# The first modulation on VectorE and rows of TensorE, and a first product that begins with half its channels

## The chip, the cores and the metric

The kernel runs on one core of a Trainium2 chip. The metric is device time in microseconds (us). Three timed runs of the kernel before gave 3132.72, 3133.52 and 3138.29; their median is 3133.52 us. One more execution was profiled, and all rows below are of that one. Engines are named as in the profile: PE is TensorE (PEld its weight loads), DVE is VectorE, ACT is ScalarE, POOL is GpSimd, SP is SyncE, which issues the loads. A line number such as L418 is that of the kernel before.

## The reference

Two transformer blocks run over 512 tokens of 1024 channels. Only the first steps of the first block matter here:

```
mod = silu(c) @ w_ada + b_ada            # w_ada: 1024 x 6144
sh1, sc1, g1, sh2, sc2, g2 = split(mod, 6)
h = layer_norm(x) * (1 + sc1) + sh1
z, xbc, dt, ... = split(h @ w_in, ...)   # the mixer's first product
```

All of it is float32. `sh1` and `sc1` are the first 2048 of the 6144 columns of `mod`: a vector of 1024 numbers times a matrix of 1024 x 2048, 8 MB of weights. After it come the mixer (a state-space scan and a short convolution), an expert layer, and the second block.

## The kernel before

**Layout.** `hT` holds the modulated activations with channels on partitions: eight chunks k of 128 channels by 512 tokens. For exactness each float32 operand of a big product is split into a high part `hi` and a rest `lo`, and a product is three matmuls (L220 to L222: hi by hi, lo by hi, hi by lo). `split` (L191, L192) makes them: ACT casts, and DVE (or another engine, `eng`) subtracts. `W.get` loads a weight block in two halves of 512 KB into `raw` (3 buffers) and splits each; a half holds four of the eight chunks. `lin_a(w, m, act)` adds up the eight chunks of 128 output channels: 24 matmuls of 128 x 512.

**The first stage** (L385 to L509) is a scope in which the order on DVE, ACT, POOL and PE is the order in which the program writes the operations; SP's loads and all that comes after the scope are placed by a planner. The stage takes statistics of the four token tiles of x, normalises each and turns it with PE transposes into `xnT` (`turn_x`), computes `sh1` and `sc1`, modulates (`modulate`: `hfull` on DVE or POOL, `hhi` on ACT, then `hlo` on DVE) and computes the first product, two times `lin_a` with the same weights (`first`, L495).

**The modulation's matrix** is worked off in four units of 512 columns, class `Ada`, in the order 0, 2, 1, 3. Units 0 and 2 give shift and scale of chunks 0 to 3, units 1 and 3 those of chunks 4 to 7. A unit loads its 1024 x 512 weights as four tiles of 512 KB (`w_ada`, 8 buffers); a tile has two of the eight chunks of rows. `part(n)` takes a tile: of the eight chunks, three are scaled by ACT and summed by POOL (`suma`), four are summed by DVE (`sumb`, L416 and L418), and one (the seventh) goes to PE straight. PE adds over the partitions with small matmuls that have 128 weights by 128 columns as the loaded operand and one column moving (`columns`, L425; four, which show as eight instructions, per tile or sum). `total` does so for the two sums, and `end` adds the three contributions on DVE (L436) and the bias (L438).

The units are interleaved: `total` and `end` of a unit stand behind `part(0)` and `part(1)` of the next (L478 to L489). Chunks 0 to 3 are modulated in the turn in which unit 1 is the new one (`j == 1`), after unit 2's `end`. Chunks 4 to 7 follow the last `end`, and then PE has the whole first product. Its weights' rest `lo` is subtracted on POOL (`eng=G`, L491).

Later, units of the remaining modulation are done beside the mixer; of these, some end in a row product (L320: one weight column, 512 columns moving).

Of the kernel before, what the change touches and what calls it, by code (L numbers as in the profile page):

```python
# [10 lines left out]
F32 = mybir.dt.float32  # L11
# [3 lines left out]
AF = mybir.ActivationFunctionType  # L15
OP = mybir.AluOpType
# [8 lines left out]
KT = 8  # L25
# [113 lines left out]
def body(tc, ins, out, stop=None, dump=None):  # L139
# [10 lines left out]
    def dma(dst, src):  # L150
        return nc.sync.dma_start(dst, src)

    with top:
# [4 lines left out]
        def psum(tag="mm", bufs=4, shape=(128, 512)):  # L158
            return pp.tile(list(shape), F32, tag=tag, bufs=bufs, name=tag)
# [34 lines left out]
        class W:  # L194
            def __init__(self, st, raw=3, hl=4, own=True, **kw):
                self.p = pool(st, "wts", **kw)
                self.rp = self.p if own is True else own.rp
                self.raw, self.hl = raw, hl

            def half(self, src, eng=V):  # L200

                r = self.rp.tile([128, 1024], F32, tag="raw", bufs=self.raw, name="raw")
                dma(r, src)
                hi = self.p.tile([128, 1024], F32R, tag="hi", bufs=self.hl, name="hi")
                lo = self.p.tile([128, 1024], F32R, tag="lo", bufs=self.hl, name="lo")
                split(r, hi, lo, eng)
                return hi, lo

            def get(self, src, n=KT, eng=V):

                out = [], []
                c = 2048 // n
                for a in range(2):
                    for t, o in zip(self.half(src[:, a * 1024:(a + 1) * 1024], eng), out):
                        for k in range(n // 2):
                            o.append(t[:, k * c:(k + 1) * c])
                return out

        def mm3(ps, lh, ll, rh, rl, start, stop):
# [4 lines left out]
        def lin_a(w, m, act, nk=KT, ps=None, k0=0, stop=True):  # L224

            ps = psum() if ps is None else ps
            for k in range(k0, nk):
                s = slice(m * 128, (m + 1) * 128)
                mm3(ps, w[0][k][:, s], w[1][k][:, s], act[0][k], act[1][k], k == 0,
                    stop and k == nk - 1)  # L230
            return ps
# [153 lines left out]
        with ExitStack() as st:  # L385
            p = pool(st, "p0", side="right")
            E = mybir.EngineType
            st.enter_context(tc.manual_schedule(engines={E.DVE, E.Activation, E.Pool, E.PE}))
            x0 = []
            for i in range(NT):  # L390
                t = p.tile([128, D], F32, name=f"x{i}")
                dma(t, ins["x"][i * 128:(i + 1) * 128, :])
                x0.append(t)

            class Ada:


                def __init__(self, j):
                    self.j, self.raw, self.n = j, [], 0
                    for n in range(4):  # L400
                        self.raw.append(p.tile([128, 2, 512], F32, name="w_ada", bufs=8))
                        dma(self.raw[n], ins["w_ada"][j, n // 2][:, n % 2 * 2:n % 2 * 2 + 2, :])
                    self.sums = [p.tile([128, 512], F32, name="sum" + n, bufs=2) for n in "ab"]

                def part(self, n):
                    (a, b), r = self.sums, self.raw[n]
                    for k in range(2):
                        c, x = cs1[:, n * 2 + k:n * 2 + k + 1], r[:, k, :]
                        if n * 2 + k == 6:
                            self.columns(x, c)  # L410
                        elif k == 0 and n < 3:
                            S.activation(x if n else a, x, AF.Copy, scale=c)
                            if n:
                                G.tensor_add(a, a, x)
                        elif n == 0:
                            V.tensor_scalar(b, x, c, None, op0=OP.mult)  # L416
                        else:
                            V.scalar_tensor_tensor(b, x, c, b, op0=OP.mult, op1=OP.add)  # L418

                def columns(self, x, c):  # L420

                    if not self.n:
                        self.ps = psum("sm", 2)
                    for a in range(4):
                        PE.matmul(self.ps[:, self.n * 4 + a:self.n * 4 + a + 1],  # L425
                                  x[:, a * 128:(a + 1) * 128], c, start=True, stop=True)
                    self.n += 1

                def total(self):
                    for t in self.sums:  # L430
                        self.columns(t, ones[:, 0:1])

                def end(self):
                    j = self.j
                    dst = (sc1 if j > 1 else sh1)[:, j % 2 * 4:j % 2 * 4 + 4]
                    V.tensor_reduce(dst, self.ps[:, :self.n * 4].rearrange("p (n a) -> p a n", a=4),  # L436
                                    AX.X, OP.add)
                    V.scalar_tensor_tensor(dst, dst, float(j > 1), bcol1[:, j * 4:(j + 1) * 4],  # L438
                                           op0=OP.add, op1=OP.add)

            mvs = p.tile([128, NT, 2], F32, name="mvs")
            for i in range(NT):
                st_ = p.tile([128, 2, 6], F32, name="bn0", bufs=2)
                for a in range(2):
                    V.bn_stats(st_[:, a, :], x0[i][:, a * 512:(a + 1) * 512])
                V.bn_aggr(mvs[:, i, :], st_)
            rs = rsqrt(p, mvs[:, :, 1], NT, 1.0, LN_EPS)
            xnT = p.tile([128, KT, T], F32, name="xnT")

            def turn_x(i):  # L450
                xn = p.tile([128, D], F32, name="xn0", bufs=2)
                V.tensor_scalar(xn, x0[i], mvs[:, i, 0:1], rs[:, i:i + 1],
                                op0=OP.subtract, op1=OP.mult)
                for kh in range(2):
                    ps = psum("tr", 2)
                    for k in range(4):
                        PE.transpose(ps[:, k * 128:(k + 1) * 128],
                                     xn[:, (kh * 4 + k) * 128:(kh * 4 + k + 1) * 128], ident)
                    S.copy(xnT[:, kh * 4:kh * 4 + 4, i * 128:(i + 1) * 128],
                           ps.rearrange("p (k t) -> p k t", k=4))  # L460

            def modulate(k):
                f = p.tile([128, T], F32, name="hfull", bufs=3)
                a, b = sc1[:, k:k + 1], sh1[:, k:k + 1]
                (G if k % 2 else V).tensor_scalar(f, xnT[:, k, :], a, b, op0=OP.mult, op1=OP.add)
                S.activation(hhi[k], xnT[:, k, :], AF.Identity, scale=a, bias=b)
                return f

            def modulated(ks):
                fs = [modulate(k) for k in ks]  # L470
                for k, f in zip(ks, fs):
                    V.tensor_sub(hlo[k], f, hhi[k].bitcast(F32))

            u = Ada(0)
            for n in range(4):
                u.part(n)
                turn_x(n)
            for j in (2, 1, 3):  # L478
                last, u = u, Ada(j)
                u.part(0)  # L480
                last.total()
                u.part(1)
                last.end()
                u.part(2)
                if j == 1:
                    modulated((0, 1))
                u.part(3)
                if j == 1:
                    modulated((2, 3))  # L489
            u.total()  # L490
            first_w = w.get(ins["w_in"][0], eng=G)  # L491
            u.end()
            modulated((4, 5))
            modulated((6, 7))
            first = [lin_a(first_w, a, hT) for a in range(2)]  # L495

            cw = sc_p.tile([128, 32, 5], F32, name="cw")
            dma(cw, ins["conv_w"])
            nrm = sc_p.tile([128, 16], F32, name="nrm")
            dma(nrm, ins["ssd_norm"])  # L500
            hd = sc_p.tile([128, 2, 32], F32, name="hd")
            load_row(hd[:, 0, :], ins["ssd_dt_bias"])
            load_row(hd[:, 1, :], ins["ssd_A_log"])
            wdt = p.tile([128, KT, 32], F32, name="wdt")
            dma(wdt, ins["w_dt"])
            V.tensor_scalar_mul(cw, cw, 0.5)
            wdh = sc_p.tile([128, KT, 32], F32R, name="wdh")
            wdl = sc_p.tile([128, KT, 32], F32R, name="wdl")
            split(wdt, wdh, wdl)  # L509
# [674 lines left out]
        with ExitStack() as st:  # L1184
# [38 lines left out]
            def rows(e):  # L1223
                return G.value_load(cnt[0:1, e:e + 1], min_val=0, max_val=T)
# [747 lines left out]
```

## Time and profile before

| | us |
|---|---|
| median of three timed runs | 3133.52 |
| the profiled execution | 3115.28 |
| its span, first to last instruction | 3113.3 |
| busy in the span: PE | 2872.3 |
| DVE | 2119.6 |
| ACT | 1501.2 |
| POOL | 856.5 |

The busy times are shares of the whole span and say little about a stage. The stage of the change takes the first 62 us; a table of stretches and the timeline of each engine show what it waits for. In a timeline a row gives start, duration, engine, line, operation, output and inputs, and in brackets how long the engine had been idle and what ended that. Rows of the same kind in a run are merged (x8), and durations of neighbours on an engine overlap a little.

### The profile page before, as it was taken

What the parts mean: (1) busy time and instruction counts of PE and PEld (TensorE: products, weight loads), DVE (VectorE), ACT (ScalarE), POOL (GpSimd) and SP (SyncE); (2) the same over time, 40 slices, a digit from 0 to 9 for tenths busy, and PEclk for the clock granted to TensorE, in tenths of its full rate; (3) what the DMA queues carried; (4) which work ended last, traced back from release to release, by engine and by line L of the source; (5) the groups of instructions that cost most, each with busy time, mean ns of one, the idle gap of its engine ahead of it and who ended that gap; (6) DMA issues with size and microseconds to landing.
All of it is one profiled execution on the core that took longest, in us unless ns stands there. A gap on an engine that the chain in (4) does not pass through costs nothing. (4 is left out here: it accounts for less than half of the span.)

```text
span 3113.3 us, 42594 instructions
## 1 busy us (share of the span) xinstructions
PE 2872.3 (92%) x14412; PEld 2356.3 (76%) x14412; DVE 2119.6 (68%) x3694; ACT 1501.2 (48%) x2524; POOL 856.5 (28%) x792
## 2 busy tenths in 40 slices
PE   6999999999878999889999399998999999899998
PEld 5888887887767777777777377687888877688886
DVE  7887887455587988786767668665555664774445
ACT  4443342455327877686666344644333425652222
POOL 3212212478352323232222402423100231310002
PEclk8999999999989999999999699999999998999999
DMA  6212414576448999998989323313333374232221
GB/s 240 81 69 97 161 67 155 200 241 227 146 150 290 323 320 327 315 334 274 308 282 292 105 92 113 105 65 138 135 122 109 103 257 147 84 129 94 89 88 68
DMA packets 143492, 540.45 MB, mean 174 GB/s; under 512 B 24320, under 2 KB 37632, under 8 KB 118528
## 3 DMA queue, kind: packets, MB, share of 16 engines
q1 hardware_dynamic: 106832, 422.21, 38.2%
q0 software_dynamic: 36272, 113.48, 13.0%
q8 instruction: 193, 3.16, 0.4%
q14 instruction: 195, 1.60, 0.2%
HBM read 509.43 MB, written 36.35 MB: 175 GB/s over the span
## 5 line engine op out<-in xcount | busy, mean ns | idle before, releaser
L192 DVE TENSOR_TENSOR lo<-raw,hi 128x1024 fp32r<-128x1024 f32 x679 | 841.7, 1266 | 337.0 <-ACT hi L191 329.8
L191 ACT CAST hi<-raw 128x1024 fp32r<-128x1024 f32 x697 | 715.9, 1053 | 576.4 <-PE mm L222 228.0
L221 PE MATMUL mm<-hlo,hi 128*128 128x512 f32 (+1 forms) x1400 | 517.3, 370 | 7.4 <-DVE hlo L962 7.4
L220 PE MATMUL mm<-hhi,hi 128*128 128x512 f32 (+1 forms) x1400 | 521.9, 373 | 1.7 <-ACT hhi L961 1.4
L222 PE MATMUL mm<-hhi,lo 128*128 128x512 f32 (+1 forms) x1400 | 517.0, 369 | 4.9 <-DVE lo L192 4.9
L220 PEld LDWEIGHTS mm<-hhi,hi 128*128 128x128 f32 x1400 | 269.4, 192 | 51.3 <-issue 5.2
L221 PEld LDWEIGHTS mm<-hlo,hi 128*128 128x128 f32 x1400 | 269.3, 192 | 50.8 <-DVE hlo L962 7.6
L222 PEld LDWEIGHTS mm<-hhi,lo 128*128 128x128 f32 x1400 | 269.0, 192 | 49.5 <-DVE lo L192 6.7
L220 PE MATMUL mm<-hi,xh 128*128 128x512 f32 x584 | 235.9, 404 | 16.2 <-ACTq L1415 8.2
L222 PE MATMUL mm<-hi,xl 128*128 128x512 f32 x584 | 231.9, 397 | 1.2 <-DVE xl L1265 1.2
L221 PE MATMUL mm<-lo,xh 128*128 128x512 f32 x584 | 229.9, 394 | 0.0
L355 POOL TENSOR_TENSOR ada_acc<-ada_acc,ada_w 128x512 f32<-128x512 f32 x112 | 168.4, 1504 | 212.0 <-ACT ada_acc L353 171.1
L220 PE MATMUL mm<-hi,fh 128*128 128x512 f32 x512 | 200.6, 392 | 5.6 <-ACT fh L191 3.4
L221 PE MATMUL mm<-lo,fh 128*128 128x512 f32 x512 | 200.4, 391 | 2.6 <-DVE lo L192 2.6
L222 PE MATMUL mm<-hi,fl 128*128 128x512 f32 x512 | 200.4, 391 | 0.0
L1220 POOL DMA_INDIRECT Rd<-ey,tt x73 | 121.7, 1667 | 242.8 <-ACT ey L1302 72.6
L1215 POOL DMA_INDIRECT x<-h2d,tt x69 | 92.2, 1337 | 333.9 <-PE mm L221 132.7
L220 PE MATMUL mm<-hi,hhi 128*128 128x256 f32 (+1 forms) x512 | 161.5, 315 | 7.3 <-ACT k L1864 7.3
L1809 DVE TENSOR_TENSOR res<-mm,gr 128x512 f32<-128x512 f32 x64 | 44.2, 691 | 180.5 <-PE mm L222 180.5
L222 PE MATMUL mm<-hi,hlo 128*128 128x256 f32 (+1 forms) x512 | 162.4, 317 | 0.0
L221 PE MATMUL mm<-lo,hhi 128*128 128x256 f32 (+1 forms) x512 | 160.6, 314 | 0.0
L220 PE MATMUL mm<-hi,ah 128*128 128x512 f32 x338 | 142.1, 420 | 6.8 <-ACT ah L1289 4.3
(815 smaller groups left out, 5860.1 us busy)
## 6 DMA issues: line engine op xcount, KB each, us to landing
raw<-in_w_gu SPq DMA_DIRECT2D x128, 1024.0 KB, 7.6
raw<-in_w_dn SPq DMA_DIRECT2D x64, 1024.0 KB, 7.5
raw<-in_mlp_w SPq DMA_DIRECT2D x128, 512.0 KB, 3.5
raw<-in_w_in SPq DMA_DIRECT2D x88, 512.0 KB, 3.6
ada_w<-in_ada_w POOLq DMA_DIRECT2D x64, 512.0 KB, 4.7
ada_w<-in_w_ada POOLq DMA_DIRECT2D x64, 256.0 KB, 3.3
ada_w<-in_ada_w POOLq DMA_DIRECT2D x64, 256.0 KB, 4.5
raw<-in_b_w_in SPq DMA_DIRECT2D x24, 512.0 KB, 4.8
```

Of the source, the lines that this page charges most:

```text
L191: S.copy(hi, raw)
L192: eng.tensor_sub(lo, raw, hi.bitcast(F32))
L220: PE.matmul(ps, lh, rh, start=start, stop=False)
L221: PE.matmul(ps, lh, rl, start=False, stop=False)
L222: PE.matmul(ps, ll, rh, start=False, stop=stop)
L355: G.tensor_add(acc, acc, x)
L1215: G.indirect_dma_start(out=buf[0:n, :], out_offset=None, in_=h2d, in_offset=index(b, e, n), bounds_check=T - 1, oob_is_err=False)
L1220: G.indirect_dma_start(out=Rd, out_offset=index(b, e, n), in_=y[0:n, :], in_offset=None, compute_op=OP.add)
L1809: V.tensor_mul(t[:, c], ps[n], g[:, c])
```

## The change

A unit no longer uses ACT and POOL. DVE sums the first five chunks into one tile (`asum`). PE takes the sum and the other three chunks with row products: one column of weights, 512 columns moving, four products into one PSUM row. `end` copies that row to SBUF with ACT, turns it into four columns with four PE matmuls of one partition, and adds the bias on DVE. `w_ada` has 10 buffers.

The order is changed too. Each unit's `end` stands right behind its last part. The halves of the first weights are loaded after the first two units' tiles and ahead of those of units 1 and 3, and are split with DVE in place of POOL, one half between the modulations of chunks 0, 1 and 2, 3, the other behind unit 1's parts. The first product is done in two pieces: chunks 0 to 3 (12 matmuls for each of the two outputs) around unit 3's first parts, chunks 4 to 7 at the end. `W.half` is divided into `load` and `halves`, with no other effect.

```diff
+                    self.sum = p.tile([128, 512], F32, name="asum", bufs=2)
+
+                def row(self, c, x, stop=False):
+                    start = self.ps is None
+                    if start:
+                        self.ps = psum("sm", 2)
+                    PE.matmul(self.ps[0:1, :], c, x, start=start, stop=stop)
 
                 def part(self, n):
...
+                    for k in range(n * 2, n * 2 + 2):
+                        c, x = cs1[:, k:k + 1], self.raw[n][:, k % 2, :]
+                        if k == 0:
+                            V.tensor_scalar(self.sum, x, c, None, op0=OP.mult)
+                        elif k < 5:
+                            V.scalar_tensor_tensor(self.sum, x, c, self.sum, op0=OP.mult, op1=OP.add)
                         else:
...
+                            if k == 6:
+                                self.row(ones[:, 0:1], self.sum)
+                            self.row(c, x, stop=k == 7)
+
+                def end(self):
+
+                    j = self.j
+                    r = p.tile([1, 512], F32, name="arow", bufs=2)
+                    S.copy(r, self.ps[0:1, :])
+                    q = psum("tr", 2)
                     for a in range(4):
...
+                        PE.matmul(q[:, a:a + 1], r[0:1, a * 128:(a + 1) * 128], ones[0:1, 0:1],
+                                  start=True, stop=True)
                     dst = (sc1 if j > 1 else sh1)[:, j % 2 * 4:j % 2 * 4 + 4]
...
+                    V.scalar_tensor_tensor(dst, q[:, :4], float(j > 1), bcol1[:, j * 4:(j + 1) * 4],
                                            op0=OP.add, op1=OP.add)
...
-            u = Ada(0)
+            u0, u2 = Ada(0), Ada(2)
             for n in range(4):
-                u.part(n)
+                u0.part(n)
                 turn_x(n)
-            for j in (2, 1, 3):
-                last, u = u, Ada(j)
-                u.part(0)
-                last.total()
-                u.part(1)
-                last.end()
-                u.part(2)
-                if j == 1:
-                    modulated((0, 1))
-                u.part(3)
-                if j == 1:
-                    modulated((2, 3))
-            u.total()
-            first_w = w.get(ins["w_in"][0], eng=G)
-            u.end()
+            u0.end()
+            raw = [w.load(ins["w_in"][0][:, a * 1024:(a + 1) * 1024]) for a in range(2)]
+            u1, u3 = Ada(1), Ada(3)
+            for n in range(4):
+                u2.part(n)
+            u2.end()
+            first_w = [], []
+            modulated((0, 1))
+            w.rows(first_w, w.halves(raw[0]), KT)
+            modulated((2, 3))
+            for n in range(4):
+                u1.part(n)
+            w.rows(first_w, w.halves(raw[1]), KT)
+            u1.end()
+            first = [lin_a(first_w, 0, hT, nk=4, stop=False)]
+            for n in range(4):
+                u3.part(n)
+                if n == 1:
+                    first.append(lin_a(first_w, 1, hT, nk=4, stop=False))
+            u3.end()
             modulated((4, 5))
             modulated((6, 7))
-            first = [lin_a(first_w, a, hT) for a in range(2)]
+            first = [lin_a(first_w, a, hT, ps=first[a], k0=4) for a in range(2)]
```

## Rows read from the trace of the kernel before

**Rows 1.** The page: busy time of the engines, and the span in 40 slices (busy tenths of PE).

```profile
PE 2872.3 (92%) x14412; PEld 2356.3 (76%) x14412; DVE 2119.6 (68%) x3694; ACT 1501.2 (48%) x2524; POOL 856.5 (28%) x792
...
PE   6999999999878999889999399998999999899998
```

**Rows 2.** The table of stretches: from and to, length, busy time (and instructions) of PE, PEld, DVE, ACT and POOL, granted clock, busy share of the DMA engines, GB/s.

```profile
26.00:48.50 22.50, 14.10 (x64) 13.84 (x65) 19.91 (x20) 8.35 (x12) 16.00 (x10) 0.51 0.72 245
48.50:54.00 5.50, 5.50 (x14) 4.34 (x15) 4.79 (x11) 4.41 (x8) 4.16 (x5) 0.50 0.03 7
54.00:62.30 8.30, 8.30 (x38) 6.68 (x37) 5.63 (x9) 2.77 (x3) 0.67 (x2) 1.00 0.62 198
62.30:840.00 777.70, 766.31 (x3918) 635.52 (x3917) 549.56 (x947) 321.37 (x521) 290.01 (x304) 0.99 0.43 147
```

**Rows 3.** The list of waits, of 14 to 54 us and, last, of PE from 55 to 840 us: who waited for whom, us in total, times, the longest.

```profile
PE sm L425 <- DVE sumb L418: 6.1, 2, 5.6
...
DVE sc L436 <- PE sm L425: 2.0, 1, 2.0
...
DVE sh L436 <- PE sm L425: 1.1, 1, 1.1
...
PE sm L320 <- DVE ada_acc L290: 4.2, 2, 2.3
```

**Rows 4.** The timeline of DVE in the first stage, with one row of ACT ahead.

```profile
12.18 0.72 ACT L412 ACTIVATE suma<-w_ada,cs 128x512 f32<-128x512 f32 x1 [8.35 <-DMA w_ada<-in_w_ada]
...
15.00 0.48 DVE L416 TENSOR_SCALAR sumb<-w_ada,cs 128x512 f32<-128x512 f32 x1
15.39 0.81 DVE L452 TENSOR_SCALAR xn<-x,mvs,rs_y 128x1024 f32<-128x1024 f32 x1
...
31.82 0.16 DVE L438 SCALAR_TENSOR_TENSOR sc<-sc,bcol 128x4 f32<-128x4 f32 x1
...
33.21 1.51 DVE L472 TENSOR_TENSOR hlo<-hfull,hhi 128x512 fp32r<-128x512 f32 x2
...
39.73 2.57 DVE L416 TENSOR_SCALAR sumb<-w_ada,cs 128x512 f32<-128x512 f32 x1
42.34 2.71 DVE L418 SCALAR_TENSOR_TENSOR sumb<-w_ada,cs,sumb 128x512 f32<-128x512 f32 x1
...
45.16 0.16 DVE L438 SCALAR_TENSOR_TENSOR sh<-sh,bcol 128x4 f32<-128x4 f32 x1
45.24 1.53 DVE L418 SCALAR_TENSOR_TENSOR sumb<-w_ada,cs,sumb 128x512 f32<-128x512 f32 x2
...
48.94 0.16 DVE L438 SCALAR_TENSOR_TENSOR sc<-sc,bcol 128x4 f32<-128x4 f32 x1
...
49.98 1.47 DVE L472 TENSOR_TENSOR hlo<-hfull,hhi 128x512 fp32r<-128x512 f32 x2 [0.30 <-ACT hhi L466]
...
52.01 1.51 DVE L472 TENSOR_TENSOR hlo<-hfull,hhi 128x512 fp32r<-128x512 f32 x2
```

**Rows 5.** The timeline of POOL.

```profile
39.39 5.11 POOL L192 TENSOR_TENSOR lo<-raw,hi 128x1024 fp32r<-128x1024 f32 x2
...
52.33 1.84 POOL L278 DMA_DIRECT2D ada_w<-in_w_ada  x3
```

**Rows 6.** The timeline of PE and of its weight loads.

```profile
18.04 1.57 PEld L457 LDWEIGHTS tr<-cst,xn 128*128 128x128 f32 x8 [0.22 <-ACT xnT L459]
...
21.86 0.94 PEld L457 LDWEIGHTS tr<-cst,xn 128*128 128x128 f32 x8
...
22.88 0.95 PE L425 MATMUL sm<-cst,suma 128*128 128x1 f32 x8
...
24.58 1.03 PE L425 MATMUL sm<-cs,w_ada 128*128 128x1 f32 x8
...
28.01 1.86 PE L425 MATMUL sm<-cst,suma 128*128 128x1 f32 x8 [2.40 <-POOL suma L414]
...
48.56 0.77 PE L220 MATMUL mm<-hhi,hi 128*128 128x512 f32 x1
...
55.50 0.40 PE L220 MATMUL sm<-hhi,wdh 128*32 128x512 f32 x1
...
62.10 0.39 PE L222 MATMUL mm<-hhi,lo 128*128 128x512 f32 x1
```

**Rows 7.** The row product of the later modulation, L320: the line's instructions (duration in ns, least, median and largest) and two of them in the timeline.

```profile
L320 PE MATMUL sm<-ada_acc,cst x32: 589/591/617, 293.5 to 2589.4; 128*1 128x512 f32 x32
...
293.46 1.02 PE L320 MATMUL sm<-ada_acc,cst 128*1 128x512 f32 x2
```

**Rows 8.** Groups by line in the first 60 us: busy time, mean ns of one, idle time before them.

```profile
L459 ACT COPY xnT<-tr 128x512 f32<-128x512 f32 x8 | 4.5, 586 | 5.3 <-PE tr L457 5.2
...
L192 DVE TENSOR_TENSOR lo<-raw,hi 128x1024 fp32r<-128x1024 f32 x2 | 2.5, 1226 | 0.2 <-ACT hi L191 0.2
...
L414 POOL TENSOR_TENSOR suma<-suma,w_ada 128x512 f32<-128x512 f32 x8 | 11.3, 1420 | 22.0 <-ACT w_ada L412 21.3 <-POOL suma L414 0.5
```

**Rows 9.** The table of stretches again, 2 us each, columns as in rows 2.

```profile
10.00:12.00 2.00, 0.00 (x0) 0.00 (x0) 1.97 (x5) 0.00 (x0) 0.00 (x0) 1.00 1.02 410
...
26.00:28.00 2.00, 0.00 (x0) 0.00 (x0) 1.97 (x2) 1.49 (x3) 1.92 (x3) 0.66 1.01 383
...
32.00:34.00 2.00, 2.00 (x11) 2.00 (x11) 1.90 (x3) 1.92 (x3) 1.49 (x1) 0.50 0.96 309
```

More of the change, by code (lines that the diff above doesn't have):

```diff
@@ L198, in __init__, with load, half, halves @@
                 self.raw, self.hl = raw, hl
-            def half(self, src, eng=V):
+            def load(self, src):
                 r = self.rp.tile([128, 1024], F32, tag="raw", bufs=self.raw, name="raw")
                 dma(r, src)
+                return r
+            def half(self, src, eng=V):
+                return self.halves(self.load(src), eng)
+            def halves(self, r, eng=V):
                 hi = self.p.tile([128, 1024], F32R, tag="hi", bufs=self.hl, name="hi")
@@ L207, in half, with rows @@
                 return hi, lo
+            def rows(self, out, ts, n):
+                c = 2048 // n
+                for t, o in zip(ts, out):
+                    for k in range(n // 2):
+                        o.append(t[:, k * c:(k + 1) * c])
             def get(self, src, n=KT, eng=V):
                 out = [], []
-                c = 2048 // n
                 for a in range(2):
-                    for t, o in zip(self.half(src[:, a * 1024:(a + 1) * 1024], eng), out):
-                        for k in range(n // 2):
-                            o.append(t[:, k * c:(k + 1) * c])
+                    self.rows(out, self.half(src[:, a * 1024:(a + 1) * 1024], eng), n)
                 return out
@@ L398, in __init__ @@
                 def __init__(self, j):
-                    self.j, self.raw, self.n = j, [], 0
+                    self.j, self.raw, self.ps = j, [], None
                     for n in range(4):
-                        self.raw.append(p.tile([128, 2, 512], F32, name="w_ada", bufs=8))
+                        self.raw.append(p.tile([128, 2, 512], F32, name="w_ada", bufs=10))
                         dma(self.raw[n], ins["w_ada"][j, n // 2][:, n % 2 * 2:n % 2 * 2 + 2, :])
-                    self.sums = [p.tile([128, 512], F32, name="sum" + n, bufs=2) for n in "ab"]
@@ L405, in part @@
-                def part(self, n):
[L406 to L416, printed above, removed]
-                        else:
-                            V.scalar_tensor_tensor(b, x, c, b, op0=OP.mult, op1=OP.add)
@@ L420, in columns @@
[L420 to L431, printed above, removed]
+                    self.sum = p.tile([128, 512], F32, name="asum", bufs=2)
@@ L433, in end @@
                 def end(self):
                     j = self.j
+                    r = p.tile([1, 512], F32, name="arow", bufs=2)
+                    S.copy(r, self.ps[0:1, :])
+                    q = psum("tr", 2)
+                    for a in range(4):
+                        PE.matmul(q[:, a:a + 1], r[0:1, a * 128:(a + 1) * 128], ones[0:1, 0:1],
+                                  start=True, stop=True)
                     dst = (sc1 if j > 1 else sh1)[:, j % 2 * 4:j % 2 * 4 + 4]
-                    V.tensor_reduce(dst, self.ps[:, :self.n * 4].rearrange("p (n a) -> p a n", a=4),
-                                    AX.X, OP.add)
@@ L438, in end @@
-                    V.scalar_tensor_tensor(dst, dst, float(j > 1), bcol1[:, j * 4:(j + 1) * 4],
+                    V.scalar_tensor_tensor(dst, q[:, :4], float(j > 1), bcol1[:, j * 4:(j + 1) * 4],
                                            op0=OP.add, op1=OP.add)
```

## The prediction

> **What bounds the kernel now.** I read the page first: PE is busy 92% of the span, and its slices are at 8 or 9 from the second on, but for two [rows 1]. A table by stretch then shows that this begins at 48.5 us: from 62.3 to 840 us PE works 766.3 of 777.7 us [rows 2]. So a microsecond by which the mixer's first product comes later should come out as a microsecond of the span, and all that counts is when PE gets through that product. Only the first 62 us are touched by the change. There PE is not the limit: from 26 to 48.5 us it works 14.1 of 22.5 us, at a granted clock of 0.51, while DVE works 19.9 and POOL 16.0 [rows 2].
>
> In the list of waits the reader should see that each unit's end hands over twice: PE waits for the sums (6.1 us, two waits), and DVE waits for PE (`sc` 2.0 us, `sh` 1.1) [rows 3]. DVE's waits are short, because it has operations of the next unit between a unit's sum and its end. The DVE timeline shows what DVE pays instead: a scale that takes 0.48 us at 15.0 takes 2.57 at 39.73, and a fused multiply-add that takes 0.74 at 45.24 (two in 1.53) takes 2.71 at 42.34 [rows 4], just beside the two splits on POOL, 39.39 to 44.50 [rows 5]. The last modulation column is written at 49.1 us [rows 4]. PE starts the first product at 48.56 [rows 6], 0.42 us a matmul at half clock until 54 (13 and a column matmul in 5.5 us), then 0.22 (38 in 8.3) [rows 2], and issues its 48th at 62.10; one matmul of the dt product (55.50) stands among them [rows 6]. The product is through at 62.3, or 62.1 without that one. I use 0.23 below, for the gaps between outputs.
>
> **The change, part by part.** The span is 3113.3 and the profiled execution 3115.3 us, 2.0 more; the sum is made against 3115.3. I lay out the new order on each engine, since DVE, ACT, POOL and PE take their instructions there as written.
>
> *Prices.* A unit's sum on DVE is one scale and four dependent multiply-adds: 0.52 + 4 x 0.78 = 3.64 us (durations of 0.48 and 0.74 plus 0.04 between dependent ones, [rows 4]), without POOL beside it. A row product (one column of weights, 512 fp32 columns moving) exists at L320: each product is two instructions of 0.59, which overlap (two in 1.02, so 0.43 apart): 0.86 us a product at full clock [rows 7]. At half clock the trace has none; the mixer's matmuls go from 0.22 to 0.42 [rows 2], about double, so 1.72. The four little matmuls that turn the row into columns are eight instructions, as those of L425: 0.95 us at full, 1.86 at half clock [rows 6]. The copy of the row from PSUM: 0.59, as L459 [rows 8]. The tail of a unit, from its sum to its written column, is then 3 rows + copy + columns + addition (0.16) + some 0.5 for five hand-overs: 2.6 + 0.6 + 0.95 + 0.16 + 0.5 = 4.8 us at full clock, 8.3 at half, 7.3 with the rows at half and the columns at full.
>
> *What it adds: a wait on DVE at each unit's end.* The addition in `end()` now stands on DVE in front of the next unit's sum, and it waits for rows, copy and columns. Everything of DVE queues behind it, and PE and ACT wait for DVE.
> - Unit 0: DVE starts at 15.0 as before; its sum is there at 15.0 + 3.64 + two normalisations of 0.73 = 20.1, the other two are done at 21.6. PE still has a row, 8 transposes, three rows and 8 transposes: 4 x 0.86 + 2 x 0.95 = 5.3 from 20.5, so 25.8; the last copy of transposes, the row's copy and the columns make it 28.3. DVE stands idle for 6.6 us.
> - Unit 2: sum at 28.3 + 3.6 = 32.0. PE has only one row to do from 28.1 and then nothing for 3 us; I let the clock fall there (below): tail 7.3, column at 39.3. Before: 31.98 [rows 4].
> - Chunks 0 to 3 and the first split: 2.7 us for two chunks as from 31.98 to 34.72 [rows 4], 1.2 for the split, 2.0 for the next two: 5.9, so 45.1. Unit 1: sum at 48.7, tail 7.3 (the second split, 1.2, lies under it): 56.0. Before: 45.3.
> - PE then does 24 matmuls of the first product, 24 x 0.23 = 5.5, and unit 3's four rows, 3.4, before the copy, columns and addition (2.0): last column at 66.7. DVE's sum of unit 3 (56.0 to 59.7) is hidden under the 24 matmuls.
> - The rest: before, hlo of chunks 4 and 5 was done 2.4 us after the last column, that of 6 and 7 4.4 us after it (49.1 to 51.45 and 53.52 [rows 4]); then 3 matmuls of chunk 7 and the 12 of the second output: 4.4 + 15 x 0.23 = 7.9. The product is through at 66.7 + 7.9 = 74.6.
>
> *What it removes.* ACT's scalings of 0.72 [rows 4], POOL's 8 additions of 1.42 [rows 8] and its two splits, 5.1 together [rows 5], all with the slowing of DVE, and 96 column instructions of PE. These savings are in the times above already, since I took DVE's undisturbed durations; DVE takes over the two splits at 1.23 each [rows 8].
>
> *Loads.* The bytes are the same. Tiles of 512 KB come at 410 GB/s, 1.27 us each (the DMA engines are full, 1.02, from 10 to 12 us), and at worst at 309 GB/s, 1.7 us (32 to 34) [rows 9]. The first tile is taken at 12.18 [rows 4], so 16 tiles and the two halves of `w_in` have landed by 12.2 + 17 x 1.27 = 33.8, at worst 41. The halves now stand in SP's queue ahead of units 1 and 3 and land by some 24 us. With 10 buffers the eleventh tile waits for unit 0's first (16.4), the last two for unit 2's first two (30.5). DVE wants unit 1 at 45 and unit 3 at 56: hidden, with over 4 us to spare; if that cover went, each late tile would cost 1.3 to 1.7. The small loads behind them in SP's queue come at about the times of before.
>
> *The clock.* It is 1.00 early on, 0.66 in 26 to 28 and 0.50 in 32 to 34 [rows 9]; it fell with the column matmuls over at 25.6 and PE idle till 28.0 [rows 6], stayed at half under more column matmuls, and was full again from 54, after some 5 us of mixer matmuls [rows 2]. The new order leaves PE idle from 29 to 32 and from 40 to 48.7, so I put the rows of units 2 and 1 at half clock and what follows at full. If it never fell, units 2 and 1 would have tails of 4.8 and the product would be through at 69; if it stayed low to the end of unit 3's rows, some 7 us more than mine.
> The Trainium skill (TensorE: Matmul & The Clock Gate, HAM oscillation) says that idle gaps between bursts of matmuls let the clock fall back to half, which speaks against this order; rows 9 agree, and by it the sum is mine, 74.6. The same page (Part 4: PE-mode transpose) says that transposes do not count as busy for the clock; here eight transpose loads took 1.57 us at 18.04 and 0.94 at 21.86 with little but transposes between [rows 6], so the measurement decides and unit 0's rows are at full clock; by the rule unit 0 would end 3.4 later.
>
> *Sum.* 74.6 - 62.1 = +12.5 us: 3115.3 + 12.5 = 3127.8, +0.40%. The three timed runs have a median of 3133.5, 18.2 above the profiled one; with the same shift that gives 3146.0. The two bounds: clock never low, 69 - 62 = +7; clock low throughout, about +20. On its way to the end the shift could shrink: PE has 11.4 us of idle between 62.3 and 840 [rows 2], the longest for `ada_acc` (4.2, two waits [rows 3]), whose loads start after this stage, at 52.33 [rows 5], and shift with it. I take all of it, with 4 as what could be swallowed.
>
> **Rivals.**
> - *Overlap (faster).* If DVE were not held at the ends (units' ends taken behind the next sums, as before), the four sums, the normalisations, the 5.9 us of chunks 0 to 3 with a split, and the other split make 15.0 + 14.6 + 2.9 + 5.9 + 1.2 = 39.6, a last tail of 4.8 gives 44.4, and the product is through at 52.3: -9.8 us, 3123.7 on the timed scale. For it: DVE's slowed operations go. Against: the order is written, and DVE's trace of before follows it exactly, even into waits [rows 3, 4]. It decides by the time for which DVE is held beyond that: under 9.8 us in all the change is faster, over that slower; I count 22.
> - *Holes refilled or clock kept (same).* The planner may put matmuls of the second weight block on chunks 0 to 3 (24 x 0.23 = 5.5 us) into PE's holes; with the clock kept up as well the rest is +7 - 5.5 = +1.5, 3135. For it: one dt matmul was pulled ahead at 55.50 [rows 6]. Against: PE's 5.6 us hole of before [rows 3] was not filled.
> - *Clock low throughout:* over +20, 3154 and more.
>
> **Chances.** Forecast (+6.3 to +20) 0.67, low clock beyond it 0.10, same 0.16, faster 0.07. A difference of 0.2%, 6.3 us, is about what can be told from none: slower 0.77, same 0.16, faster 0.07. The range, +0.5 to +20 us, is 3134 to 3154: it leaves out about a tenth on either side, the overlap below and the low clock above. The forecast alone has 3140 to 3154.
>
> **What would show it.** DVE idle of about 6 us before the addition of unit 0's `end()` and as much at units 2 and 1; the modulation's columns written at about 28, 39, 56 and 67 us; a granted clock of 0.5 in part of 29 to 55; PE's first product starting near 56, seven microseconds later than before, and through near 75. It is wrong if the DVE queue takes the next unit's sum before the addition, if a row product takes far from 0.86 or 1.72 us, or if the mixer starts late and the span doesn't follow.

## The result, and the profile after

The changed kernel takes 3150.53 us (median of 6 runs, 3145.28 to 3158.72), the kernel before 3130.09 beside it (6 runs, 3121.01 to 3138.29): a ratio of 1.0063, 95% interval 1.0044 to 1.0082. It is slower, as forecast, and 3150.5 lies inside the range; the forecast of 3146.0 was 4.5 us low. The profiled execution took 3147.95 us (span 3145.9).

The page of the changed kernel answers to [rows 1]: PE's share of the span is 92% again, so the page alone doesn't show where the time is.

```profile
PE 2881.3 (92%) x14380; PEld 2345.1 (75%) x14380; DVE 2117.5 (67%) x3696; ACT 1497.4 (48%) x2516; POOL 837.5 (27%) x782
```

The table of stretches does; first the three of [rows 2], then shorter ones (from and to, length, busy time and instructions of PE, PEld, DVE, ACT and POOL, granted clock, DMA share, GB/s).

```profile
26.00:48.50 22.50, 9.96 (x33) 3.13 (x31) 11.54 (x18) 8.59 (x13) 2.22 (x2) 0.70 0.52 177
48.50:54.00 5.50, 4.51 (x6) 0.60 (x6) 4.56 (x7) 0.41 (x1) 0.00 (x0) 0.50 0.43 107
54.00:62.30 8.30, 7.58 (x34) 5.47 (x34) 3.57 (x6) 0.86 (x2) 0.00 (x0) 0.92 0.35 125
...
28.00:30.00 2.00, 1.87 (x10) 0.92 (x10) 1.01 (x3) 0.00 (x0) 0.00 (x0) 1.00 0.91 363
30.00:32.00 2.00, 0.00 (x0) 0.00 (x0) 1.89 (x4) 0.00 (x0) 0.00 (x0) 0.87 0.33 102
32.00:38.00 6.00, 5.28 (x6) 0.59 (x6) 0.66 (x1) 0.00 (x0) 0.00 (x0) 0.50 0.80 234
...
42.00:54.00 12.00, 4.51 (x6) 0.60 (x6) 10.67 (x15) 4.91 (x7) 0.97 (x1) 0.50 0.32 94
...
56.00:62.00 6.00, 6.00 (x29) 4.88 (x29) 3.57 (x6) 0.00 (x0) 0.00 (x0) 1.00 0.16 65
```

From 26 to 48.5 us DVE was busy for 19.9 us before and for 11.5 after, POOL for 16.0 and for 2.2, PE for 14.1 and for 10.0: all three do less, and the stage is longer. From 32 to 38 us six instructions of PE at a clock of 0.50 are all that the core computes, but for the end of DVE's sum. The timeline of DVE says why (the bracket is its idle time before the instruction and what ended it):

```profile
28.96 0.16 DVE L443 SCALAR_TENSOR_TENSOR sh<-tr,bcol 128x4 f32<-128x4 f32 x1 [7.33 <-PE tr L440]
29.04 0.48 DVE L425 TENSOR_SCALAR asum<-w_ada,cs 128x512 f32<-128x512 f32 x1
29.55 3.11 DVE L427 SCALAR_TENSOR_TENSOR asum<-w_ada,cs,asum 128x512 f32<-128x512 f32 x4
39.74 0.16 DVE L443 SCALAR_TENSOR_TENSOR sc<-tr,bcol 128x4 f32<-128x4 f32 x1 [7.08 <-PE tr L440]
40.02 0.55 DVE L470 TENSOR_SCALAR hfull<-xnT,sc,sh 128x512 f32<-128x512 f32 x1
...
46.33 3.11 DVE L427 SCALAR_TENSOR_TENSOR asum<-w_ada,cs,asum 128x512 f32<-128x512 f32 x4
...
56.58 0.16 DVE L443 SCALAR_TENSOR_TENSOR sh<-tr,bcol 128x4 f32<-128x4 f32 x1 [3.45 <-PE tr L440]
56.66 0.48 DVE L425 TENSOR_SCALAR asum<-w_ada,cs 128x512 f32<-128x512 f32 x1
...
67.88 0.16 DVE L443 SCALAR_TENSOR_TENSOR sc<-tr,bcol 128x4 f32<-128x4 f32 x1 [3.55 <-PE tr L440]
```

L443 is the addition in `end()`. DVE stands idle in front of it at every unit. What follows at once had been queued behind it: L425, the next unit's first operation, at units 0 and 1, and the modulation of chunks 0 to 3 (L470) at unit 2. The list of waits of 14 to 80 us adds the four up, to 21.4 us, where [rows 3] has 3.1:

```profile
DVE sh L443 <- PE tr L440: 10.8, 2, 7.3
DVE sc L443 <- PE tr L440: 10.6, 2, 7.1
```

And PE's timeline is the other side of each wait:

```profile
32.72 1.86 PE L418 MATMUL sm<-asum,cst 128*1 128x512 f32 x2 [2.85 <-DVE asum L427]
34.38 3.62 PE L418 MATMUL sm<-w_ada,cs 128*1 128x512 f32 x4
38.66 1.05 PE L440 MATMUL tr<-cst,arow 1*128 1x1 f32 x8 [0.66 <-ACT arow L437]
...
49.49 1.87 PE L418 MATMUL sm<-asum,cst 128*1 128x512 f32 x2 [8.84 <-DVE asum L427]
...
56.47 0.50 PE L229 MATMUL mm<-hhi,hi 128*128 128x512 f32 x1
...
66.79 1.05 PE L440 MATMUL tr<-cst,arow 1*128 1x1 f32 x8
...
75.70 0.39 PE L231 MATMUL mm<-hhi,lo 128*128 128x512 f32 x1
```

PE waits for a sum (2.85 and 8.84 us), then DVE waits for PE: the two hand work back and forth, and each is idle while the other works. The product's first matmul starts at 56.47 (48.56 before) and its last at 75.70 (62.10 before, [rows 6]): 13.6 us later. Thirteen matmuls of the second weight block stand among the product's here, which the planner put there.

**How far it carries.** From here on I use one measure for every run: the start of an instruction less the start of the same instruction (same engine, operation, tiles, shapes and source text) in the first profile of before; the median over 100 to 250 us, where it is flat, is called the shift. The changed kernel has a shift of 14.4, and 16.0 from 350 to 800 us: nothing is swallowed by then. It is not the 13.6 carried on, though. For what before does from 76 to 88 us the shift is 10.7, since thirteen matmuls (3.0 us) are done ahead. It comes to 14.4 behind that: at 102 to 106 us of its own time PE stands idle for 1.9 us, and then it runs at half clock:

```profile
102.00:106.00 4.00, 2.15 (x13) 1.43 (x12) 3.54 (x9) 1.93 (x6) 2.29 (x3) 1.00 0.38 131
106.60:110.00 3.40, 3.40 (x10) 2.63 (x9) 3.40 (x4) 0.75 (x2) 2.64 (x3) 0.50 0.02 5
```

The end of its span is 32.5 us later. Most of the rest, 15 us, comes between 880 and 960 us, in the routing stage, where the granted clock differs. There a look at before's own two profiles helps (the second is the control below), 900 to 940 us, first the first:

```profile
900.00:920.00 20.00, 16.54 (x126) 15.97 (x126) 11.90 (x73) 1.59 (x4) 11.54 (x13) 0.91 0.45 177
920.00:940.00 20.00, 15.94 (x103) 14.40 (x103) 10.65 (x39) 6.07 (x9) 9.46 (x10) 0.91 0.11 33
```

and then the second:

```profile
900.00:920.00 20.00, 15.43 (x82) 14.92 (x81) 8.86 (x52) 1.33 (x3) 8.98 (x10) 0.66 0.52 200
920.00:940.00 20.00, 17.48 (x109) 16.98 (x108) 11.19 (x54) 4.41 (x7) 9.10 (x10) 0.74 0.02 1
```

The same kernel was granted 0.91 once and 0.66 to 0.74 the other time, and PE did 126 matmuls or 82 in the first of these stretches. Whether the lower clock makes the stage longer or only goes with it is not shown.

### The profile page after: what moved, and what is told of

It reads as the page before. It is cut to its first block, busy times and chain, and to the rows that moved or that the text cites. A ratio compares the mean times of both kernels' runs of the same rounds, so it can differ in the third digit from the quotient of the medians.

```text
span 3145.9 us, 42497 instructions
## 1 busy us (share of the span) xinstructions
PE 2881.3 (92%) x14380; PEld 2345.1 (75%) x14380; DVE 2117.5 (67%) x3696; ACT 1497.4 (48%) x2516; POOL 837.5 (27%) x782
```

## The experiments

In the diffs `n` counts a unit's parts, and what is not shown is as in the kernel named.

**Controls.** Both kernels, unchanged.

> The kernel before, unchanged, for a second profile. Theory (of the 32.5 us between the two profiled executions, only what has built up by 300 us, 14.4, belongs to the change; the 16 us that come between 900 and 960 us, in the routing stage, are the granted clock of that execution): the first product is through at 62 us again, within 0.5, while the stretch from 880 to 960 us may differ from the first profile's by several us. Rival (the routing stage of before always runs at a granted clock near 0.91 and that of the changed kernel always near 0.8): the stretch takes the same time as in the first profile, within 2 us.

> The changed kernel, unchanged, for a second profile and a tighter time. Theory: product through at 75.7 again, within 0.5; timed 14 to 16 us over before (ratio 1.0045 to 1.0051). Rival (the routing stage belongs to the change): again some 16 us more between 880 and 960 us than in the kernel before, and timed about 30 us over before (1.0095).

Before again: the shift is 0.7, and 17.0 behind 960 us; its time is 3129.4. It loses about as much in the routing stage without any change, so the 15 us there are no part of the change. The changed kernel again: shift 13.2, timed 1.0040 of before, interval 1.0015 to 1.0065, which is 12.5 us (5 to 20; 14 to 16 were expected). The product was through at 76.1, within 0.5 of the first profile, and the shift goes from 11.1 (76 to 88 us) to 13.2 with the clock at 1.00, though the first unit's sum began 1.3 us later in this execution (15.79, not 14.52): the stage's start differs by a microsecond from run to run, and shifts under 1 us mean nothing.

**Unit 0's end taken later.**

```
-            u0.end()
...
             for n in range(4):
                 u2.part(n)
+                if n == 2:
+                    u0.end()
             u2.end()
```

> The changed kernel with the end() of unit 0 alone taken later, behind part 2 of unit 2, so that DVE has the sum of unit 2 to do while PE and ACT finish unit 0. Theory (DVE held at the ends is the cost, 7.3 us at unit 0): DVE's idle time before the addition of unit 0 falls from 7.3 to under 1 us, everything up to the product comes 7 us earlier (through at 68.7, or 66 where the clock then doesn't fall), timed about 7 us under the changed kernel, 8 over before (1.0025). Rival A (the cost is the row products and the work given to DVE, not the order): within 2 us of the changed kernel. Rival B (PE's clock eats it: the rows of unit 2 stay at half clock and start beside the columns): 3 to 4 us gained.

The shift is 5.8, so 7.4 to 8.5 us are gained by moving one addition behind five operations (its copy and columns move with it), and the product is through at 68.8, as expected. The timed runs don't show this gain: 1.0031 of before (1.0007 to 1.0055), a median of 3145.77 beside 3146.83 for the changed kernel, where 7 us were expected. Its DVE:

```profile
22.11 3.11 DVE L427 SCALAR_TENSOR_TENSOR asum<-w_ada,cs,asum 128x512 f32<-128x512 f32 x4
29.60 0.16 DVE L443 SCALAR_TENSOR_TENSOR sh<-tr,bcol 128x4 f32<-128x4 f32 x1 [4.38 <-PE tr L440]
33.98 0.16 DVE L443 SCALAR_TENSOR_TENSOR sc<-tr,bcol 128x4 f32<-128x4 f32 x1 [4.21 <-PE tr L440]
```

The expectation of idle time under 1 us was a miss: 4.4 us are left, since PE itself, with its transposes and rows, is not through with unit 0 before 28.5. The gain is there all the same, because the sum of unit 2 now lies in the wait, and unit 2's rows follow without a hole, at full clock. By the profile rivals A and B fall; by the time alone rival A would not.

**All ends later.** Each `end()` behind part 2 of the next unit, unit 1 summed ahead of chunks 0 to 3, the early product behind unit 3's rows.

```
+            for last, u in ((u0, u2), (u2, u1)):
+                for n in range(4):
+                    u.part(n)
+                    if n == 2:
+                        last.end()
             modulated((0, 1))
...
             for n in range(4):
-                u1.part(n)
+                u3.part(n)
+                if n == 2:
+                    u1.end()
...
+            first = [lin_a(first_w, a, hT, nk=4, stop=False) for a in range(2)]
             u3.end()
```

> The changed kernel with every end() behind part 2 of the next unit, unit 1 summed before the chunks 0 to 3 are modulated, and the 24 early matmuls after the rows of unit 3. Theory (the holds on DVE are the whole loss, and without them the new units are quicker than the old): DVE is busy nearly without a gap from 15 to 45 us, last column at 44 to 48 us, product through at 53 to 58, so 5 to 9 us under the kernel before (ratio 0.9972 to 0.9984) and 20 to 23 under the changed one. Rival A (the row products on PE are the loss): still slower than before, ratio over 1.002. Rival B (PE becomes the limit at half clock: four units of rows and columns, 16 transposes and 24 matmuls in 30 us): product through at 60 to 64, the same as before within 0.1%.

The shift is 1.7, timed 1.0014 (0.9988 to 1.0039): no difference from before, and far better than the changed kernel, in time too (medians of 3136.89 and 3146.83 in the same set of runs), yet it is neither the theory's 53 to 58 us (the product is through at 64.9, with 11 matmuls of the next block in it) nor the reason that rival B gave. PE ran at a clock of 1.00 up to 38 us; what was late is in its own order:

```profile
44.15 1.87 PE L418 MATMUL sm<-asum,cst 128*1 128x512 f32 x2 [4.21 <-DVE asum L427]
45.81 3.28 PE L418 MATMUL sm<-w_ada,cs 128*1 128x512 f32 x4
...
54.37 0.39 PE L231 MATMUL mm<-hhi,lo 128*128 128x512 f32 x1
54.69 1.05 PE L440 MATMUL tr<-cst,arow 1*128 1x1 f32 x8
```

A hole of 4.2 us, unit 3's rows at half clock behind it, and then its four columns behind all 24 early matmuls, 5.6 us after the row could have been copied. I had put a new wait where the old one had been.

**The old unit in the new order.** The kernel before's `Ada` (ScalarE, GpSimd and columns on PE, no row product), each `end()` still ahead of the next sum.

```
             class Ada:
...
+                def end(self):
+                    self.total()
+                    j = self.j
...
```

> The order of the changed kernel (each end() ahead of the next unit's sum, split on VectorE, early matmuls) with the unit of the kernel before (ScalarE scales, GpSimd adds, TensorE turns the sums into columns, no row). Read by the shift of the stretch from 100 to 250 us against the first profile of before, which is 14.4 and 13.2 us in the two profiles of the changed kernel and 0.7 in the second profile of before. Theory (DVE is held at the end of a unit for the chain row products, copy, columns, which the old unit has shorter: sums, columns, reduction): holds of 5, 3.5 and 3 us in place of 7.3, 7.1 and 3.5, first product through near 62 to 66, shift 0 to 4. Rival (the order by itself is the loss, whatever the unit): shift 10 to 14.

Shift 4.0, the upper edge of the theory; DVE's waits are shorter than expected but for the last:

```profile
24.13 0.17 DVE L446 TENSOR_REDUCE sh<-sm 128x4 f32<-128x12 f32 x1 [3.16 <-PE sm L434]
...
31.12 0.17 DVE L446 TENSOR_REDUCE sc<-sm 128x4 f32<-128x12 f32 x1 [1.96 <-PE sm L434]
...
45.85 0.17 DVE L446 TENSOR_REDUCE sh<-sm 128x4 f32<-128x12 f32 x1 [0.83 <-PE sm L434]
...
55.73 0.17 DVE L446 TENSOR_REDUCE sc<-sm 128x4 f32<-128x12 f32 x1 [6.75 <-PE sm L434]
```

So in the serial order the form of the unit matters for 13.8 - 4.0 = 9.8 us (13.8 is the mean of the two shifts of the changed kernel).

**PE kept at work in its holes.** Row products whose result nothing reads, 3 and 9 of them.

```
+            def warm(n):
+                q = psum("tr", 2)
+                for k in range(n):
+                    PE.matmul(q[0:1, :], cs1[:, k % 8:k % 8 + 1], x0[0][:, :512],
+                              start=k == 0, stop=k == n - 1)
...
             u0.end()
+            warm(3)
...
             u2.end()
+            warm(9)
```

> The changed kernel with row products whose result nothing uses, 3 of them on PE behind the columns of unit 0 and 9 behind those of unit 2, in the two holes in which PE waits for DVE's sums. Theory (PE's granted clock falls in these holes and the rows that follow run at 1.72 to 1.86 us in place of 0.86): the clock is 1.00 from 28 to 56 us, the three rows behind each sum take 2.6 us and not 5.3, columns at 37 and 51 us, shift from 100 to 250 us 8 to 9 us in place of 13.2 to 14.4. Rival (the clock does not follow such row products, or the added ones stand in the way of the real ones): the rows stay at 1.8 or the shift stays at 13 or more.

Shift 8.1, and the granted clock is 1.00 in every stretch from 30 to 56 us. In PE's timeline (L470 are the added products) the row products behind a sum take 2.7 us for three and not 5.3:

```profile
33.05 1.02 PE L418 MATMUL sm<-asum,cst 128*1 128x512 f32 x2 [0.28 <-DVE asum L427]
33.90 1.88 PE L418 MATMUL sm<-w_ada,cs 128*1 128x512 f32 x4
36.45 1.05 PE L440 MATMUL tr<-cst,arow 1*128 1x1 f32 x8 [0.67 <-ACT arow L437]
37.42 7.89 PE L470 MATMUL tr<-x,cs 128*1 128x512 f32 x18
```

The clock is worth 13.8 - 8.1 = 5.7 us of the loss (5.1 to 6.3 against either profile of the changed kernel); the work without a use shows no cost of its own there. The Trainium skill (TensorE: Matmul & The Clock Gate, HAM oscillation) says that gaps between bursts of matmuls drop the clock to half; the 5.28 us of row products at 0.50 in the changed kernel and their 2.7 us here agree.

**No early product.** All 48 matmuls behind the last column.

```
-            first = [lin_a(first_w, 0, hT, nk=4, stop=False)]
...
-                if n == 1:
-                    first.append(lin_a(first_w, 1, hT, nk=4, stop=False))
...
-            first = [lin_a(first_w, a, hT, ps=first[a], k0=4) for a in range(2)]
+            first = [lin_a(first_w, a, hT) for a in range(2)]
```

> The changed kernel without the early part of the first product: all 48 matmuls behind the last column, as in the kernel before. Theory (the 24 early matmuls fill a time in which PE would wait for the sum of unit 3, and cost the last column only what they stand ahead of its rows): the column is 0 to 2 us earlier, PE idles from 57 to 60 us, and the product is through 0 to 4 us later, shift 13 to 18 us. Rival (the early product is what makes the stage late, since the rows of unit 3 stand behind it): shift under 11 us.

Shift 15.3. The last column comes at 65.7, 2.3 us earlier than in the changed kernel, a little more than expected, and PE waits 2.85 us for the sum of unit 3 and begins its rows at half clock (two instructions in 1.87 at 59.35). So in this order the early product is worth some 1.5 us, about what two executions differ by: it is not the cause of the loss, and no great gain either.

**The split on VectorE alone**, in the kernel before.

```
-            first_w = w.get(ins["w_in"][0], eng=G)
+            first_w = w.get(ins["w_in"][0])
```

> The kernel before with the two splits of the first block of the mixer's weights on VectorE and not on GpSimd, nothing else. Theory (DVE's two operations of 2.6 and 2.7 us beside POOL's splits are slowed by them and cost 4.1 us ahead of the last column): these fall to 0.5 and 0.75 us, the splits take 1.2 each on DVE behind the last sum, under PE's columns; product through 1 to 3 us earlier, shift from 100 to 250 us -3 to 0. Rival (the slow operations wait for something else, or the splits on DVE delay the last column): shift over 0.7.

Shift -4.9, more than the 1 to 3 us that I gave it. The same kernel was run again, timed, beside two others:

> The kernel before with the splits on VectorE once more, timed beside the other two. Theory: shift from 100 to 250 us -4.9 again, within 0.7, and the same in the time: 0.9984 of before, with an interval that a few us of run to run difference may widen past 1. Rival (the gain is swallowed later): ratio 1.0.

Shift -5.6; timed 0.9990, interval 0.9975 to 1.0005, which doesn't part it from before. In its DVE timeline the scale and the multiply-add that took 2.57 and 2.71 us in [rows 4] take 0.47 and 0.75, and the two splits fill the wait for unit 3's columns:

```profile
39.42 0.47 DVE L416 TENSOR_SCALAR sumb<-w_ada,cs 128x512 f32<-128x512 f32 x1
39.93 0.75 DVE L418 SCALAR_TENSOR_TENSOR sumb<-w_ada,cs,sumb 128x512 f32<-128x512 f32 x1
...
42.33 2.35 DVE L192 TENSOR_TENSOR lo<-raw,hi 128x1024 fp32r<-128x1024 f32 x2
44.60 0.16 DVE L436 TENSOR_REDUCE sc<-sm 128x4 f32<-128x12 f32 x1
```

The Trainium skill (SBUF — State Buffer, 🔬 SBUF: two separate sides) calls the ports that VectorE and GpSimd share an exclusive lock, held for a whole instruction. These rows agree: beside a GpSimd split of some 2.6 us [rows 5] DVE's operation took its own 0.5 to 0.75 and 2 us more, not some per cent.

**Both units in a good order.** First the new unit, ends late, with unit 3's columns no longer behind the 24 matmuls:

```
             modulated((2, 3))
+            u1.end()
+            for n in range(3):
+                u3.part(n)
+            first = [lin_a(first_w, 0, hT, nk=4, stop=False)]
+            u3.part(3)
+            w.rows(first_w, w.halves(raw[1]), KT)
+            first.append(lin_a(first_w, 1, hT, nk=1, stop=False))
+            u3.end()
+            lin_a(first_w, 1, hT, ps=first[1], k0=1, nk=4, stop=False)
```

> The kernel with all ends late, with the end of unit 3 no longer behind the 24 early matmuls: one output's 12 stand ahead of unit 3's rows, 3 of the other's in the time in which ScalarE copies the row, 9 behind the columns; and the end of unit 1 goes ahead of unit 3. Theory (in ends_late the new units were already quick, with row products at 0.86 us up to 38 us, and what spoilt it was the last column, which stood behind 24 matmuls, and the rows of unit 3, at half clock after a hole of 4.2 us): PE has matmuls from 40 to 43 us, the rows of unit 3 take 0.86 each, last column at 48 to 49, product through at 55 to 57, shift from 100 to 250 us -5 to -7, timed 0.9976 to 0.9985 of before. Rival (the rows cannot be kept at full clock, or PE is full): last column at 51 or later, shift over -3.

Shift -5.3, last column written at 49.0; the clock was 1.00 in every stretch from 30 to 54 us, and unit 3 goes through PE like this:

```profile
44.15 1.02 PE L418 MATMUL sm<-asum,cst 128*1 128x512 f32 x2 [0.38 <-DVE asum L427]
45.00 1.88 PE L418 MATMUL sm<-w_ada,cs 128*1 128x512 f32 x4
...
47.70 1.05 PE L440 MATMUL tr<-cst,arow 1*128 1x1 f32 x8
```

Timed 0.9989, interval 0.9970 to 1.0007; nearly all of the 5.3 us are lost again later (the shift is -2.3 from 340 us on and -0.2 at 800 to 840), and why was not looked into.

Then the old unit in the order of before, with split on VectorE and early product; the loads of the first weights and the 10 buffers (not shown) are as in the changed kernel:

```
                 if j == 1:
+                    w.rows(first_w, w.halves(raw[0]), KT)
                     modulated((2, 3))
+            first = [lin_a(first_w, 0, hT, nk=4, stop=False)]
             u.total()
-            first_w = w.get(ins["w_in"][0], eng=G)
+            w.rows(first_w, w.halves(raw[1]), KT)
+            first.append(lin_a(first_w, 1, hT, nk=4, stop=False))
             u.end()
```

> The units and the order of the kernel before with the splits on VectorE, one ahead of chunks 2 and 3 and one behind the last sum, w_in's halves loaded after unit 2, and the 24 matmuls of the first product on chunks 0 to 3 around the columns of unit 3. Theory (with the split off POOL this kernel's last column comes at 45 us and the rest of the gain is to have half of the product done by then): product through at 53 to 57, shift -5 to -9, at least as good as the row products in their best order. Rival (the early matmuls at half clock, 0.42 us each, stand in front of the last columns and cost what they save): shift -5 to -1.

Shift -8.2, timed 0.9979, interval 0.9960 to 0.9997 (3113.44 us beside 3121.28): the only version that is faster than the kernel before by more than its interval, and its shift is still -7.8 at 800 to 840 us. Its time is no better than that of the split alone in the same set (3113.66), so what the early product adds is read from the shift. The rival's price was paid in part: 12 early matmuls ran at half clock, and the last column comes at 46.5, 1.1 to 1.5 later than in the two profiles with the split alone, but 12 of the product's 48 matmuls are done by then, 12 more follow up to 48.6, and PE goes on without a wait.

**What the runs add up to.** With the split on VectorE and the early product in all four:

```
shift, us           ends interleaved   ends ahead of the next sum
old unit                 -8.2                  +4.0
row products             -5.3             +14.4 and +13.2
```

From before to the changed kernel that is -5.2 for the split (mean of two profiles), -3.0 for the early product with its loads and buffers (-5.2 to -8.2), +12.2 for the order (-8.2 to +4.0) and +9.8 for the row products within it: +13.8. The order is the larger lever, and the row products cost three times as much in the bad order as in the good one (9.8 and 2.9). The 2.9 is the weaker number: the two kernels with interleaved ends differ in more than the unit, since each has the ends, the splits and the early matmuls where they suit it. Most cells are single profiles, good to about 1 us. The expectation on the old unit in the new order set "the unit" against "the order by itself"; its number came out on the unit's side, but only the interleaved pair shows that both hold: the order makes each unit's chain a wait, and the unit sets how long that is.

## Why the prediction was right

- **The wait at each end**: right in kind, and in size at units 0 and 2: 7.3 us of idle time at unit 0 (6.6 forecast) and 7.1 at unit 2 (7.3 by the tail). At unit 1 "as much" was forecast and 3.5 measured: the chain held the addition for 7.1 us there too (49.4 to 56.6), but DVE filled half of that with splits, two of them of the second weight block. The 22 counted is the last column less that of the overlap rival, 66.7 - 44.4. With the measured 68.0 it is 23.6; the 21.4 us of idle time are another sum. Unit 0's column was written at 29.1 (28.3), unit 2's at 39.9 (39.3), unit 1's at 56.7 (56.0), the last at 68.0 (66.7).
- **Prices**: a unit's sum took 3.62 us (29.04 to 32.66; forecast 3.64), three rows at half clock 5.28 (5.16), the columns 1.05 at full (0.95), the tail with rows at half clock 7.2 (7.3). The row product at half clock, which no row of before showed, was taken as double; it measured 1.76 each.
- **The clock**: it fell where forecast (0.50 in 32 to 38 and 42 to 54), and was 1.00 from 56. Unit 0's rows were at full clock (three in 2.73 us from 22.93), so the 3.4 us that the prediction weighs there did not come. The bound "clock never low", +7, was tried: 8.1.
- **Loads**: hidden, as forecast; none of DVE's waits in the stage is for a load.
- **The sum**: +12.5 forecast, 13.6 at the end of the product. 0.8 of the 1.1 comes at unit 0, though its sum began at 14.52 and not at 15.0: DVE's last normalisation waited 0.74 us for PE, and PE was through later; 0.6 at unit 3, whose chain after unit 1's column took 11.3 us and not 10.7; a little came back behind the last column. Unit 3's terms as printed (56.0 + 5.5 + 3.4 + 2.0) add up to 66.9 and not 66.7. Two things the forecast hadn't: PE did thirteen matmuls of the next block while it waited, so that behind the product the shift is 10.7, and the stretch behind it, up to 110 us, then took 3.7 more (2.1 in the second profile). That these nearly cancel, and leave 14.4 beside 12.5, is luck.
- **Swallowing**: up to 4 us were allowed; from 100 to 800 us none was found.
- **Rivals**: *overlap* didn't happen, since DVE's queue took the addition first. Its price was -9.8; the nearest run, the row products with their ends late, gives -5.3. Its last column comes at 49.0 and not at 44.4: DVE still waits 3.5 us for PE at unit 0, which the price left out, and the rest was not traced. *Holes refilled*: the planner put 4 matmuls into the wait for unit 3's row (65.66 to 66.46) and 9 behind it, none into the large holes. *Clock low throughout*: no.
- **What failed**: a size only. The forecast carried its +12.5 to the timed median; that shows +20.4, with an interval of 13.8 to 25.7, and the control 12.5 (5 to 20). The stage's 14 us fit both. That 3146.0 came within 4.5 us of the result owes something to its base: the three runs that it starts from have a median 3.4 us above that of the six, and the shift itself, 12.5 beside 20.4, was 7.9 short. I also took the profiled 3115.3 as an ordinary execution that is 18 us under the median by chance; its second profile takes 15.5 us more in one stage, the routing (from a shift of 1.5 at 880 us to 17.0 behind 960).

## What to carry to other kernels

An instruction that waits for another engine should stand in its queue behind work that is ready: here one addition of 0.16 us, five operations too early, cost 7 to 8 us of the stage. Count a rewrite that lowers the busy time of three engines by its chain of hand-overs, not by the work it saves; and where several edits come together, run them one by one, as two of these four (split and early product) were gains in the stage, hidden under the other two. If an engine's slow operations stand just beside another engine's long ones, move the other's first: that single edit was worth 5 us in the stage, though twelve timed runs did not part it from nothing.

## What the runs showed of the hardware

The granted clock in the routing stage differs between executions of one kernel (0.91, or 0.66 to 0.74, above). In the first eight profiles of the experiments, all on one chip, the shift grew by 9 to 15 us between 880 and 960 us, in the kernel before among them; in the last three, taken later and on another chip, it fell by 1 us each. Whether the chip or the hour decides was not tried.

PE at work is not PE at full clock: in the last version above PE was busy for 9.55 of 10 us, with column matmuls and, from 38.8 us, the product's first, at 0.50, and the clock rose behind the mixer's matmuls that followed (from 44 us):

```profile
30.00:40.00 10.00, 9.55 (x43) 9.27 (x43) 9.73 (x12) 6.76 (x10) 6.83 (x5) 0.50 0.73 237
40.00:44.00 4.00, 4.00 (x11) 3.13 (x10) 3.90 (x8) 0.00 (x0) 0.17 (x1) 0.50 0.02 7
44.00:48.00 4.00, 4.00 (x26) 3.56 (x26) 2.54 (x7) 1.50 (x3) 1.03 (x1) 0.96 0.57 140
```

With row products in that place, in the order above it, the clock stayed at 1.00. Why was not tried.
